# Layer 0's attention in a two-layer transformer trunk: fewer modulation blocks up to the latent heads, more beside the output product, and bias products and scores in another place of the order

## The chip, the cores and the metric

The kernel runs on one core of a Trainium2 chip. The metric is device time in microseconds of one launch; weights and activations come from the chip's memory in each launch. PE is the matrix engine (PEld its weight loads), DVE the vector engine, ACT the scalar engine, POOL the general one, SP the queue that issues the transfers.

## The reference

One sequence of 256 tokens of width 2048 goes through two layers, all in float32. A conditioning vector `c` gives each layer six vectors of 2048 (shift, scale and gate of the attention, shift, scale and gate of the MLP):

```python
cond = jax.nn.silu(c)
mod = cond @ w_ada[l] + b_ada[l]
sh_a, sc_a, g_a, sh_m, sc_m, g_m = split(mod, 6)
h = rmsnorm(x) * (1 + sc_a) + sh_a
proj = h @ w_in[l]          # dq, dk, dv (1024 each), cq 512, ckv 256, kr 64
out_a = diff_attention(dq, dk, dv, positions, bias_table, lam, ...)   # 4 heads, two softmaxes each, T5 bias
q  = rmsnorm(cq, gq) @ w_uq[l]      # 8 latent heads, 128 + 64 rotated
kv = rmsnorm(ckv, gkv) @ w_ukv[l]
out_b = mla_attention(q_nope, rope(q_rope), k_nope, rope(kr), v)
x = x + g_a * (concat(out_a, out_b) @ w_o[l])
h = rmsnorm(x) * (1 + sc_m) + sh_m
x = x + g_m * (square(relu(h @ w_mlp_in[l])) @ w_mlp_out[l])
```

A last norm ends it. `w_ada` is 2048 x 12288 per layer, 201 MB for both layers.

## The kernel before, in words

**Products.** Float32 weights are split on the way in: `weights()` loads one tile of 128 x 2048 (1 MB; a few are 128 x 1536) into one of five shared buffers `raw` (line 164), ACT copies it to `hi` in a reduced format (line 145) and DVE takes the rest, `lo` (line 146), half a tile at a time; `hi` and `lo` have four half-tiles each. A product is three passes, hi x hi, hi x lo, lo x hi (`mac`, lines 188 to 190; `tokens_by_k`, lines 259 to 261, with 512 columns a pass). Activations are split likewise. PSUM has eight banks, all from one pool.

**Modulation.** `w_ada` isn't multiplied on PE. It is cut into 192 blocks of 128 x 2048 (one block gives 128 outputs); a block is loaded into the same five `raw` buffers (`ada_load`, line 296), and one DVE pass multiplies it by the broadcast `cond` and sums the row (`ada_sums`, line 304). The blocks go in a fixed order `ada_todo`: layer 0's attention shift and scale (32), its gate (16), MLP shift and scale (32), MLP gate (16), then layer 1's in the same order. When they go is set by a *rate*: each call of `weights()` adds `self.rate` to a credit, and for each whole unit one block is loaded (`more`); its DVE pass is put behind the split of the next weight tile. In the softmax steps of layer 0's latent heads `tick` does the same with `RATE_S`. Where a value is needed and its blocks have not been loaded, `ada_need` loads and sums all up to it at that place.

**Layer 0.** `head` computes the norm and, in one loop over the 16 blocks of 128 features, the combined projection with `w_b` (latents, half of the queries and keys) into all eight PSUM banks; here the first 32 blocks of modulation are needed step by step (16 of them ahead of the loop). Products with the other queries, keys and the values were done for the first eight feature blocks before (`w_f1`, `w_v1`); `rest_feats` (`w_f2`) and `val(cg, 2)`, `val(cg, 3)` (`w_dv`) do the rest. Then, in `layer`: `latent` norms a latent; `bias_marks(a)` makes eight marks `oh` per query block a on ACT and DVE, and `bias_products(a, marks)` multiplies them by the bias table (lines 527, 528), for a = 2 and 3 here; `rope_setup` and `keys` make the rotated key; `probs(hd)` computes the two softmaxes of a differential head (scores at line 1041), `turn` transposes them; `up_k`, `up_q`, `up_r`, `up_v` are the products that go up from the latents. The list `mla` holds the three steps of each latent head (scores and softmax, transpose, values) in a staggered order, with a `tick` behind each of its ten groups. The output product follows: `w_oa` in four tiles, `w_ob` in twelve, then the norm and the product with `w_n0` (`norm_then_by_k`, 16 tiles in eight steps), then the MLP.

**What sets the order.** Each engine has one queue. Inside `manual_schedule(engines={PE})` PE's order is the written one: so in `head` and in the MLP. Elsewhere, so in all of layer 0's attention and its output product, a planner orders the instructions by simulated times, with the written order as its preference. Transfers are all issued from SP, in one order; a transfer into a `raw` buffer waits until the buffer's last reader on DVE is through.

Of the kernel before, what the change touches and what calls it, by code (L numbers as in the profile page):

```python
# [21 lines left out]
NK = D // P  # L22
# [71 lines left out]
NSPLIT = 8  # L94
# [3 lines left out]
NNORM = 12  # L98


RATE_H, RATE_A0, RATE_S, RATE_O, RATE_A1, RATE_A2, RATE_K, RATE_M = 1.25, 1.2, 1.3, 0.6, 0.5, 0.7, 0.6, 0.66


class Trunk:
# [261 lines left out]
    def head(self):  # L366
# [63 lines left out]
        self.part_v = [[flat(self.copy(ps, "pvp")) for ps in y] for y in vals]  # L430
        self.rate = RATE_H
        banks = self.open_banks(8)
        for k in range(NK):
            for i, w in enumerate(self.weights(io["w_b"][0, k])):
                for j in range(8):
                    b = 4 * i + j // 2
                    self.mac(banks[b][:, j % 2], w, j * P, P, h[k], k == 0 and j % 2 == 0, k == NK - 1 and j % 2 == 1, True)
            if k + 2 < NK:
                ready(k + 2)
        return h, banks  # L440

    def rest_feats(self, h, ps, banks):
# [262 lines left out]
    def layer(self, l, acc, st):  # L705
# [23 lines left out]
        def keys():  # L729
            ps = self.bank("pkr")  # L730
            self.tile_cols(ps[:, 0], io["w_kr"][l], h)
            self.kr = self.rope_k(ps[:, 0])

        def up_k():
            kn.extend(self.copy(ps, "kn") for ps in self.small(io["w_uk"][l], ckv, 8))

        def up_q(b):
            qn.extend(self.copy(ps, "qn", ms) for ps in self.small(io["w_uq"][l, b], cq, 4))
# [28 lines left out]
        def probs(hd):  # L767
            return lambda: a.append(self.diff_probs(l, hd, q[hd], kk[hd]))
# [15 lines left out]
        if l == 0:  # L784
            q += [self.copy(ps, "q", qs) for ps in banks[3:5]]
            kk += [self.copy(ps, "k", -1.0) for ps in banks[5:7]]
            q.append(self.copy(banks[7], "q", qs))
            ckv += self.latent([ckr], gkv)
            marks = self.bias_marks(2)
            banks = self.open_banks(3)  # L790
            self.rest_feats(h, (0, 1), banks)
            self.bias_products(2, marks)
            cq += self.latent(cqr, gq)
            marks = self.bias_marks(3)
            self.rope_setup()
            self.rest_feats(h, (2, 3), banks)
            k2, q3, k3 = self.rest_sums(banks)
            kk += [k2, k3]
            q.append(q3)
            self.bias_products(3, marks)  # L800
            self.lambdas()
            keys()
            probs(0)()
            up_k()
            probs(1)()
            for kq in (2, 3):
                val(0, kq)()
            probs(2)()
        else:
            def two(i, dst, scale):  # L810
                ps = self.wides([io["w_q"][0, i + j] for j in range(2)], h)
                dst.append(self.joined(ps, self.u("qk"), scale))

            two(0, q, qs)
            two(8, kk, -1.0)
            ckv += self.latent([ckr], gkv)
            for hd in range(1, HD):
                two(2 * hd, q, qs)
                probs(hd - 1)()
                two(8 + 2 * hd, kk, -1.0)  # L820
                if hd == 1:
                    cq += self.latent(cqr, gq)
            keys()
            self.rate = RATE_A2
            up_k()
        probs(3)()
        up_q(0)
        turn(0)()
        up_r()
        turn(1)()  # L830
# [6 lines left out]
        turn(3)()  # L837
        for f in mla[3:6]:
            f()
        self.interleave(  # L840
            [val(cg, kq) for cg in range(2) for kq in range(4)] if l else [val(1, kq) for kq in (2, 3)],
            mla[6:] + [av[0][0], av[1][0]],
        )
        acc = None
        g = self.mod[l, 2]
        self.ada_need(l, 2, NK - 1)
# [391 lines left out]
```

## Time and profile before

| what | value |
|---|---|
| median of 3 runs | 2251.49 us (2248.39 to 2251.86) |
| the profiled execution | 2249.45 us, its span 2247.6 us |
| PE busy | 2167.3 us, 96% of the span |
| DVE busy | 1627.8 us, 72% |
| ACT busy | 1153.5 us, 51% |
| `raw<-in_w_ada` blocks | 192 transfers of 1024 KB |
| one DVE pass over a block (line 304) | 2.28 us |
| all line 304 passes | 437.7 us of DVE |

A page of the profile shows one execution: busy times per engine, the span in forty slices, the chain of work that ended last, and groups of instructions by source line, written as output<-inputs. A wait is put down to the instruction whose semaphore came last. PE's busy time is modelled from pipelined instructions, so a full PE says that it never stood still, not that it ran at its peak.

### The profile page before, as it was taken

What the parts mean: (1) busy time and instruction counts of PE and PEld (TensorE: products, weight loads), DVE (VectorE), ACT (ScalarE), POOL (GpSimd) and SP (SyncE); (2) the same over time, 40 slices, a digit from 0 to 9 for tenths busy, and PEclk for the clock granted to TensorE, in tenths of its full rate; (3) what the DMA queues carried; (4) which work ended last, traced back from release to release, by engine and by line L of the source; (5) the groups of instructions that cost most, each with busy time, mean ns of one, the idle gap of its engine ahead of it and who ended that gap; (6) DMA issues with size and microseconds to landing.
All of it is one profiled execution on the core that took longest, in us unless ns stands there. A gap on an engine that the chain in (4) does not pass through costs nothing.

```text
span 2247.6 us, 31016 instructions
## 1 busy us (share of the span) xinstructions
PE 2167.3 (96%) x12318; PEld 1899.0 (84%) x12318; DVE 1627.8 (72%) x2168; ACT 1153.5 (51%) x1704; POOL 20.4 (1%) x43
## 2 busy tenths in 40 slices
PE   6996989999999999999999999999999999999997
PEld 4896768999888888888888888999888888888886
DVE  7898996798778777778799886678544545555555
ACT  3435546446455445445446655647545534544643
POOL 0000000000000000000001000000000000000000
PEclk9998889999999999999999999999999999999999
DMA  9897686778888888987877675675555554555551
GB/s 388 334 377 278 251 342 226 286 262 330 328 312 319 331 305 307 335 319 308 323 292 267 255 270 217 226 264 192 199 195 187 189 195 179 190 203 191 194 193 60
DMA packets 83811, 585.39 MB, mean 260 GB/s; under 512 B 9297, under 2 KB 9681, under 8 KB 17361
## 3 DMA queue, kind: packets, MB, share of 16 engines
q1 hardware_dynamic: 83666, 583.42, 69.7%
q8 instruction: 96, 1.57, 0.3%
q14 instruction: 49, 0.40, 0.0%
HBM read 581.28 MB, written 2.10 MB: 260 GB/s over the span
## 4 chain that ended last, share of the span: by engine, by line
PE 89%; DVE 7%; ACT 1%; DMA 1%; issue 1%; DVEq 0%; ACTq 0%; SPq 0%
PE ps L209 20%; PE ps L212 11%; PE py L941 10%; PE py L943 10%; PE py L939 10%; PE pk L190 2%; DVE ada L304 2%; PE pk L188 2%; PE pk L189 2%; PE ps L189 2%; PE ps L188 2%; PE ps L190 2%; DVE lo L146 1%; PE pv L259 1%; PE pv L260 1%; PE pv L261 1%
## 5 line engine op out<-in xcount | busy, mean ns | idle before, releaser
L146 DVE TENSOR_TENSOR lo<-raw,hi 128x1024 fp32r<-128x1024 f32 (+1 forms) x724 | 855.5, 1194 | 498.4 <-ACT hi L145 335.9
L145 ACT ACTIVATE hi<-raw 128x1024 fp32r<-128x1024 f32 (+1 forms) x724 | 745.4, 1036 | 708.9 <-PE py L943 373.1
L209 PE MATMUL ps<-h,hi 128*128 128x512 f32 x2016 | 472.8, 391 | 0.0
L209 PEld LDWEIGHTS ps<-h,hi 128*128 128x128 f32 x2016 | 375.1, 188 | 75.7
L304 DVE SCALAR_TENSOR_TENSOR ada<-ada,cond 128x2048 f32<-128x2048 f32 x192 | 437.7, 2282 | 0.0
L939 PE MATMUL py<-hi,hid 128*128 128x512 f32 x1024 | 326.0, 389 | 0.0
L941 PE MATMUL py<-lo,hid 128*128 128x512 f32 x1024 | 325.8, 389 | 0.0
L943 PE MATMUL py<-hi,hid 128*128 128x512 f32 x1024 | 325.7, 389 | 0.0
L212 PEld LDWEIGHTS ps<-h,lo 128*128 128x128 f32 x2016 | 250.5, 192 | 5.0
L212 PE MATMUL ps<-h,lo 128*128 128x256 f32 x2016 | 252.0, 283 | 0.0
L941 PEld LDWEIGHTS py<-lo,hid 128*128 128x128 f32 x1024 | 192.3, 188 | 40.1 <-DVE lo L146 0.4
L943 PEld LDWEIGHTS py<-hi,hid 128*128 128x128 f32 x1024 | 192.3, 188 | 39.9
L939 PEld LDWEIGHTS py<-hi,hid 128*128 128x128 f32 x1024 | 191.8, 188 | 39.2
L190 PE MATMUL pk<-h,lo 128*128 128x256 f32 x496 | 142.1, 288 | 6.9 <-DVE lo L146 6.7
L188 PE MATMUL pk<-h,hi 128*128 128x256 f32 x496 | 140.9, 286 | 3.4 <-ACT h L660 3.4
L189 PE MATMUL pk<-h,hi 128*128 128x256 f32 x496 | 141.6, 286 | 0.0
L190 PEld LDWEIGHTS pk<-h,lo 128*128 128x128 f32 x496 | 96.8, 196 | 7.9 <-DVE lo L146 7.7
L977 ACT ACTIVATE sum<-ps 128x256 f32<-128x256 f32 x110 | 42.1, 383 | 114.2 <-PE ps L212 113.6
L188 PEld LDWEIGHTS pk<-h,hi 128*128 128x128 f32 x496 | 96.2, 195 | 4.1 <-ACT h L660 3.8
L189 PEld LDWEIGHTS pk<-h,hi 128*128 128x128 f32 x496 | 96.7, 195 | 0.2
L182 DVE TENSOR_TENSOR hid<-relu,hid 128x256 fp32r<-128x256 f32 x128 | 48.3, 419 | 48.4 <-ACT hid L181 48.4
L190 PE MATMUL pa<-ah,lo 128*128 128x258 f32 x192 | 55.3, 288 | 4.6 <-DVE lo L146 4.6
(236 smaller groups left out, 2582.2 us busy)
## 6 DMA issues: line engine op xcount, KB each, us to landing
raw<-in_w_m SPq DMA_DIRECT2D x238, 1024.0 KB, 4.8
ada<-in_w_ada SPq DMA_DIRECT2D x192, 1024.0 KB, 5.0
raw<-in_w_ob SPq DMA_DIRECT2D x24, 1024.0 KB, 4.8
raw<-in_w_b SPq DMA_DIRECT2D x16, 1024.0 KB, 6.6
raw<-in_w_q SPq DMA_DIRECT2D x16, 1024.0 KB, 4.8
raw<-in_w_dv SPq DMA_DIRECT2D x12, 1024.0 KB, 4.8
raw<-in_w_n SPq DMA_DIRECT2D x16, 768.0 KB, 5.5
raw<-in_w_oa SPq DMA_DIRECT2D x8, 1024.0 KB, 5.4
```

The costliest lines, as they stand in the source:

```text
L145: nc.scalar.activation(hi, v, AF.Copy)
L146: ins = nc.vector.tensor_tensor(lo, v, hi.bitcast(F32), ALU.subtract)
L182: self.nc.vector.tensor_tensor(lo, val[:, i], hi.bitcast(F32), ALU.subtract)
L188: mm(ps, hi, x[0], start=first, stop=False, skip_group_check=shared)
L189: mm(ps, hi, x[1], start=False, stop=False, skip_group_check=shared)
L190: mm(ps, lo, x[0], start=False, stop=last, skip_group_check=shared)
L209: mm(ps.rearrange("p a b -> p (a b)"), part(w, 0, k), both, start=k == 0, stop=False)
L212: mm(ps[:, 0], part(w, 1, k), x, start=False, stop=k == nk - 1)
L304: ins = nc.vector.scalar_tensor_tensor(w, w, 1.0, self.cond, ALU.mult, ALU.mult, accum_out=acc[:, i : i + 1])
L939: mm(o, xh[:, tok], hi[:, part[j]], start=start, stop=False)
L941: mm(o, xh[:, tok], lo[:, part[j]], start=False, stop=False)
L943: mm(o, xl[:, tok], hi[:, part[j]], start=False, stop=stop)
```

## The change

It does five things.

- Rates: `RATE_A0` (layer 0's attention) from 1.2 to 0.35, `RATE_S` (ticks) from 1.3 to 0.75, `RATE_O` (its output product) from 0.6 to 1.1.
- In the head's loop the rate is set to zero once the first 32 blocks have been loaded.
- The first products after the head: `rest_feats` for the first two pairs goes ahead of the key latent's norm and the marks of query block 2; the bias product of block 2 goes behind the sums of `rest_feats`, and the query latent's norm and the marks of block 3 behind it.
- `val(0, 2)` and `val(0, 3)` go ahead of the marks' product of block 3, and `val(1, 2)`, `val(1, 3)` between the scores of the differential heads; `up_q(0)` goes between scores, too. So the last steps of the latent heads no longer have the two value products among them.
- For layer 1 nothing changes (the two lines for `probs(3)` and `up_q(0)` moved into its branch).

```diff
-RATE_H, RATE_A0, RATE_S, RATE_O, RATE_A1, RATE_A2, RATE_K, RATE_M = 1.25, 1.2, 1.3, 0.6, 0.5, 0.7, 0.6, 0.66
+RATE_H, RATE_A0, RATE_S, RATE_O, RATE_A1, RATE_A2, RATE_K, RATE_M = 1.25, 0.35, 0.75, 1.1, 0.5, 0.7, 0.6, 0.66
...
         banks = self.open_banks(8)
+        rest = len(self.ada_todo) - 2 * (NK - NSPLIT)
         for k in range(NK):
...
                 ready(k + 2)
+            if len(self.ada_todo) <= rest:
+                self.rate = 0.0
         return h, banks
...
             q.append(self.copy(banks[7], "q", qs))
+            banks = self.open_banks(3)
+            self.rest_feats(h, (0, 1), banks)
             ckv += self.latent([ckr], gkv)
             marks = self.bias_marks(2)
-            banks = self.open_banks(3)
-            self.rest_feats(h, (0, 1), banks)
-            self.bias_products(2, marks)
-            cq += self.latent(cqr, gq)
-            marks = self.bias_marks(3)
-            self.rope_setup()
             self.rest_feats(h, (2, 3), banks)
             k2, q3, k3 = self.rest_sums(banks)
             kk += [k2, k3]
             q.append(q3)
+            self.rope_setup()
+            self.bias_products(2, marks)
+            cq += self.latent(cqr, gq)
+            val(0, 2)()
+            marks = self.bias_marks(3)
+            val(0, 3)()
+            keys()
+            self.lambdas()
             self.bias_products(3, marks)
-            self.lambdas()
-            keys()
+            up_k()
             probs(0)()
-            up_k()
+            val(1, 2)()
             probs(1)()
-            for kq in (2, 3):
-                val(0, kq)()
+            up_q(0)
             probs(2)()
+            val(1, 3)()
+            probs(3)()
         else:
...
             up_k()
-        probs(3)()
-        up_q(0)
+            probs(3)()
+            up_q(0)
         turn(0)()
...
-        self.interleave(
-            [val(cg, kq) for cg in range(2) for kq in range(4)] if l else [val(1, kq) for kq in (2, 3)],
-            mla[6:] + [av[0][0], av[1][0]],
-        )
+        light = mla[6:] + [av[0][0], av[1][0]]
+        if l:
+            self.interleave([val(cg, kq) for cg in range(2) for kq in range(4)], light)
+        else:
+            for f in light:
+                f()
```

## The prediction

> **What bounds the kernel now.** I read the page's engine shares and its forty slices first, to see where the matrix engine is not full.
>
> ```profile
> span 2247.6 us, 31016 instructions
> PE 2167.3 (96%) x12318; PEld 1899.0 (84%) x12318; DVE 1627.8 (72%) x2168; ACT 1153.5 (51%) x1704; POOL 20.4 (1%) x43
> ...
> PE   6996989999999999999999999999999999999997
> DVE  7898996798778777778799886678544545555555
> PEclk9998889999999999999999999999999999999999
> ```
>
> PE works nearly everywhere but in slices 4 to 6 (some 170 to 340 us), where it falls to 6 tenths and its granted clock falls too, while DVE stands at 9. This is layer 0's attention. So I cut the time from 87 to 531 us at the stages' own borders (first to last product of each, from the order of time): the combined input projection to 182, attention to 355.4, output product to 457, the product with `w_n0` to 531. Columns: length, busy time (count) of PE, PEld, DVE, ACT, POOL, granted clock, DMA share, GB/s. The rows with one engine are those of line 304 alone, the pass that makes modulation from one block of `w_ada`; its count holds each pass and its read-out, so x64 is 32 blocks.
>
> ```profile
> 87.00:182.00 95.00, 92.90 (x768) 92.09 (x767) 83.21 (x99) 40.35 (x51) 0.00 (x0) 1.00 0.93 362
> 182.00:214.00 32.00, 25.29 (x168) 23.94 (x168) 30.58 (x42) 19.24 (x28) 0.00 (x0) 0.89 0.79 285
> 214.00:224.00 10.00, 0.00 (x0) 0.00 (x0) 10.00 (x19) 3.49 (x6) 0.00 (x0) 0.60 0.33 118
> 224.00:293.00 69.00, 57.47 (x308) 48.34 (x308) 64.24 (x133) 37.48 (x71) 0.81 (x1) 0.84 0.72 268
> 293.00:355.40 62.40, 52.53 (x262) 44.40 (x262) 57.71 (x100) 34.87 (x80) 0.00 (x0) 0.95 0.84 322
> 386.00:457.00 71.00, 70.66 (x581) 69.75 (x579) 54.31 (x64) 29.90 (x35) 0.00 (x0) 1.00 0.78 282
> 457.00:531.00 74.00, 70.67 (x576) 70.67 (x577) 63.88 (x89) 37.20 (x56) 0.00 (x0) 0.98 0.80 291
> 182.00:355.40 173.40, 135.30 (x737) 116.68 (x738) 162.53 (x291) 95.08 (x183) 0.81 (x1) 0.87 0.75 282
> ...
> 182.00:355.40 173.40, 73.02 (x64) 0.87 0.75 282
> 386.00:457.00 71.00, 16.05 (x14) 1.00 0.78 282
> 457.00:531.00 74.00, 20.63 (x18) 0.98 0.80 291
> ```
>
> Attention takes 173.4 us, in which DVE works 162.5 (94%) and PE 135.3. Of DVE's time 73.0 us are the 32 blocks, which this stage does not need: 2.28 us each. In the output product PE is full and DVE has 17 us to spare; in the product with `w_n0` it has 10. The list of waits between 181 and 355.4 us says what PE stood for (us, times, longest):
>
> ```profile
> PE pb L527 <- DVE oh L516: 11.2, 1, 11.2
> PE pk L190 <- DVE lo L146: 6.0, 1, 6.0
> PE psm L1108 <- DVE qr L1019: 4.9, 1, 4.9
> PE psc L1041 <- DVE mx L1042: 4.7, 3, 3.6
> PE pqr L1014 <- ACT qr L278: 4.0, 1, 4.0
> PE pt L1059 <- ACT sm L1112: 3.3, 2, 3.0
> ```
>
> Nearly all end in DVE. The longest is the bias product of query block 3: its marks (`oh`) come after the latent's norm on DVE, and no other product is at hand. The clock costs as well: busy time by granted clock over the four parts is 25.3 x 0.89 + 57.5 x 0.84 + 52.5 x 0.95 = 121 us at full clock, against 135.3.
>
> **The change, part by part.** *How many blocks move.* The rates add up call by call in the code. Before, the head's 16 weight tiles at 1.25 issue 20 blocks; the attention's 14 tiles at 1.2 and ten ticks at 1.3 issue 29 (three of the head's are summed here, which makes the 32 seen). After, the head stops at 16; 14 x 0.35 + 10 x 0.75 with a credit of 0.25 issue 12, and `ada_need(0, 2, 15)` ahead of the output product forces the four still missing of its gate: 16. Output product: 16 tiles at 0.6 give 10, at 1.1 they give 18. The `w_n0` stage: 9 by rate in both, but only 18 of the 32 blocks of shift and scale are there when it starts, so the last two of its eight steps force three each: 15.
>
> *Attention, DVE.* 162.5 - 73.0 + 16 x 2.29 = 126 us. *PE* at full clock is 121. So the bound is no longer one engine, and what counts is how the two overlap. The end of the stage I take by itself, because `val(1, 2)` and `val(1, 3)` no longer run between its heads. The stretch before the output product where that is already so:
>
> ```profile
> 331.00:350.00 19.00, 14.38 (x72) 11.61 (x71) 16.84 (x38) 14.71 (x36) 0.00 (x0) 0.98 0.77 297
> ...
> 331.00:350.00 19.00, 7.73 (x8) 0.98 0.77 297
> ...
> 332.71 0.59 PE L1107 MATMUL psm<-kn,qn 128*128 128x256 f32 x2
> ...
> 344.81 0.59 PE L1107 MATMUL psm<-kn,qn 128*128 128x256 f32 x2
> ```
>
> From the first to the seventh of these half-head scores are 12.1 us, so 4.0 us a head, with 7.7 us of blocks (3.4 passes) in 19 us: about what the new rate issues. Five heads have their scores in the new tail: 20 us, and from the last score (344.8) to 355.4 another 10. Tail: 30 us, with PE busy 23 of them and DVE 27, by this row's shares. The four forced blocks come in the tail too, 9.2 us of DVE ahead of the first `w_oa` split: nothing if they fit the drain, 9.2 if they all delay it; I take 5, the middle, since DVE has only 11% free in that row. What is left for the stage ahead of the tail is PE 121 - 23 = 98, DVE 126 - 27 - 9 = 90. With 10% for waits (before, DVE, the bound then, lost 7%, and now both are close) 108. Sum 108 + 35 = 143, against 173.4: **-30 us**. Ends: perfect overlap, 98 + 30 = 128, gives -45; if only the first two waits of the list go, -17.
>
> *The moved order.* Marks, bias products, norm of the query latent and scores each get a product behind which they can wait: the 11.2 us of `pb` is covered by `val(0, 2)` and the rest products. Cover gone, that wait comes back. Only in the head does PE follow the written order; in this section a planner lays out the instructions by simulated times, so the written order is no more than a preference. It is priced inside the 10%. `probs(3)` and `up_q(0)` in the other branch stay where they were: nothing for layer 1.
>
> *Head.* Four blocks fewer at its end. PE is idle 2.1 of 95 us there; the wait of 6.0 right after it, for a weight tile that was late, is inside the attention's sum. -1 us (0 to -2).
>
> *Output product.* From 386 to 457 are 12 tiles: 13 blocks instead of 7 make DVE 54.3 + 6 x 2.29 = 68 of 71 us. Its transfers grow to 25 of 1024 KB in 71 us, some 370 GB/s. The nearest rows for such density are the head's own 87 to 182 (20 blocks beside 16 tiles) and its middle:
>
> ```profile
> 60.00:80.00 20.00, 20.00 (x73) 13.64 (x72) 14.55 (x23) 6.03 (x12) 0.00 (x0) 1.00 1.00 419
> 120.00:155.00 35.00, 35.00 (x294) 35.00 (x294) 30.64 (x39) 12.24 (x14) 0.00 (x0) 1.00 0.97 387
> ...
> raw<-in_w_n SPq DMA_DIRECT2D x16, 768.0 KB, 5.5
> ...
> ada<-in_w_ada SPq DMA_DIRECT2D x192, 1024.0 KB, 5.0
> ```
>
> PE was full over 35 us at 387 GB/s, and 419 was reached. The head's idle 2.1 and the late tile's 6.0 make 8 the upper end; 0 is the lower, and I take **+3**, nearer the full row because this density is a little lower. The five shared buffers of tiles and blocks are the link: a later block waits on SP for DVE to free one, and the next tile is queued behind it.
>
> *`w_n0` stage.* 63.9 + 6 x 2.29 = 77.6 us of DVE in 74: 3.6 over. And they are not spread: without blocks a step costs DVE (63.9 - 20.6) / 8 = 5.4, with 4.2 blocks 15.0, against 70.67 / 8 = 8.8 of PE, so 6.2 over in each of the last two, 12 together, less what DVE is ahead (two tiles' worth, at most 8.8). Between +3 and +12, I take **+6**, nearer the plain excess of 3.6. In bytes: 12.6 MB of `w_n` and 15 blocks, 28.3 MB in 74 us, 382 GB/s, under both rows above.
>
> The Trainium skill says otherwise: in "DMA: Bandwidth & Descriptors", section "Where 436 GB/s comes from", transfers from HBM are held to about 358 GB/s per core. By that figure the two stages' 64 MB would need 179 us instead of 175.6, so 3 us more, and the sum would be -19 and the time 2232 us. The two rows above, 387 and 419, do not agree with it, and I leave it out of the sum.
>
> *Later stages.* Three blocks fewer are done when the MLP starts; its rate of 0.66 is the same, no need is missed, and the three are made up in layer 1's output product, where blocks now run on at the same rate for some tiles longer than before. A row of that place:
>
> ```profile
> 1470.00:1500.00 30.00, 30.00 (x253) 30.00 (x252) 25.35 (x29) 13.01 (x14) 0.00 (x0) 1.00 0.82 297
> ```
>
> PE is full there with blocks running, so 0; without that cover 3 x 2.29 = 7 us.
>
> **Sum.** -30 - 1 + 3 + 6 = -22 us. Span 2247.6 to 2225.6. The profiled execution took 2249.45, so 2227; the runs' median, 2251.49, lies 2.0 above that, and less 22 it gives **2229 us**.
>
> **Rivals.**
> (1) *More is won*: the two engines overlap nearly fully, -40 to -45, and the later stages give back only 5. For it: layer 1's attention, at a rate of 0.5, with its four value products between the heads:
>
> ```profile
> 1306.00:1420.00 114.00, 113.21 (x649) 98.47 (x648) 82.50 (x137) 65.55 (x122) 0.00 (x0) 1.00 0.64 239
> ```
>
> PE idles 0.8 of 114 us. Against: DVE is at 72% there, here it would be near 90%. Time 2212.
> (2) *Waits take the place of waits*: the bias marks or the rotated queries stay late, the bare tail goes chain-bound with the clock dropping (0.60 where PE stood still). The stage gains the lower end's 17, the later stages cost 9: 2243. For it: 16.9 us of the waits listed are on scores, rotation and softmax, and a block still stands ahead of them on DVE now and then.
> (3) *Slower: the blocks cost more where they go than they did here.* In the output product and `w_n0` stage a block stands between two weight splits on DVE, the tile behind it waits for a buffer, PE waits for the tile. It decides from a loss of 31 us over 32 tiles, 1.0 us a tile; at 1.3 a tile the time is 2262. For it: DVE at 96% and more in both. Against: the head, as dense, lost 8.1 over 16 tiles, half a microsecond a tile.
> (4) *It does not do what it says*: the planner puts products and marks back as they were. Then the order is worth nothing, but 16 blocks fewer still shorten DVE's queue; it ends in (2), or, with more given back, within 4.5 us of before.
>
> **How the numbers follow.** Likeliest case (2215 to 2237) 0.55; rival 1 0.13; rival 2 with 4's first half 0.17; no change, within 0.2% (4.5 us, about what a measurement of this kernel tells from no change) 0.05; slower 0.10. Hence faster 0.85. The range from 2211 to 2247 holds the likeliest case, rival 2 and about half of rival 1.
>
> **What would show it.** Right: attention about 143 us with 16 blocks of line 304 in it, the `pb` wait gone, granted clock above 0.95; PE idle a few us in the output product; an idle stretch of PE in the last two steps of `w_n0`, waiting for `lo` or `h`. Wrong: attention still above 155 us with PE waiting on softmax or rotation; PE idle over 15 us between the output product's first tile and the MLP; or a DMA share of 1.0 with PE waiting there.

## The result, and the profile after

The changed kernel takes 2253.68 us (median; 2252.25 to 2257.56) against 2250.93 for the kernel before on the same chip: ratio 1.0014, 95% interval 1.0008 to 1.0021. That is inside the 0.2% which the prediction called no change. It forecast 2229 with a range of 2211 to 2247, so the measured time lies outside. The profiled execution took 2253.18 us.

The page of the kernel after, the lines that answer to those shown of before (TensorE is PE in the rows, VectorE DVE, ScalarE ACT):

```profile
span 2251.4 us, 31003 instructions
PE 2173.8 (97%) x12318; PEld 1899.5 (84%) x12318; DVE 1628.3 (72%) x2168; ACT 1152.5 (51%) x1704; POOL 17.8 (1%) x43
...
PE   6998989898999999999999999999999999999997
DVE  7886987898777877777899886688544545555555
PEclk9998999999999999999999999999999999999999
```

Slice 4 has risen from 6 to 8 tenths of PE, but slices 8 and 10 (394 to 450 and 507 to 563 us), which stood at 9, are at 8. Busy time by stage (columns as in the prediction; first all engines, then line 304 alone, whose count is twice the blocks):

```profile
182.00:340.20 158.20, 134.20 (x733) 111.69 (x731) 127.91 (x250) 92.81 (x179) 0.81 (x1) 0.91 0.58 213
340.20:451.00 110.80, 102.87 (x814) 100.52 (x812) 91.44 (x113) 49.13 (x79) 0.00 (x0) 0.97 0.81 295
451.00:532.40 81.40, 74.05 (x577) 73.15 (x578) 73.30 (x97) 35.15 (x54) 0.00 (x0) 0.94 0.89 341
505.00:532.40 27.40, 20.37 (x145) 19.67 (x146) 24.14 (x33) 12.75 (x22) 0.00 (x0) 0.88 1.00 401
...
182.00:340.20 158.20, 38.86 (x34) 0.91 0.58 213
340.20:451.00 110.80, 38.85 (x34) 0.97 0.81 295
451.00:532.40 81.40, 34.15 (x30) 0.94 0.89 341
```

The later two stages before, cut at the same events (first `w_oa` product, first `w_n0` product, first wide product of the MLP):

```profile
355.40:460.30 104.90, 101.25 (x814) 99.12 (x812) 74.46 (x94) 50.05 (x78) 0.00 (x0) 1.00 0.69 251
460.30:531.00 70.70, 70.67 (x576) 70.67 (x577) 61.08 (x86) 36.24 (x54) 0.00 (x0) 0.98 0.81 293
```

The attention (182 us to the first `w_oa` product) is 15.2 us shorter. The output product with its norm gives back 5.9, the `w_n0` stage 10.7, and what follows is 2.4 longer (1719.0 against 1716.6): -15.2 + 5.9 + 10.7 + 2.4 = +3.8, the difference of the spans. What TensorE waited for in the kernel after, first between 181 and 340 us, then between 340 and 533:

```profile
PE pn L588 <- DVE acc L579: 5.8, 1, 5.8
PE psm L1117 <- DVE qr L1028: 4.8, 1, 4.8
PE psm L1116 <- DVE sm L1118: 4.5, 5, 1.6
PE pb L530 <- DVE oh L519: 4.2, 4, 2.6
...
PE pk L188 <- ACT h L663: 10.1, 3, 5.0
PE ps L188 <- ACT hi L145: 2.6, 1, 2.6
```

(`pn` is the product that sums a norm's squares, `pb` the bias product, `psc` the scores of the differential heads, `psm` those of the latent heads, `pk` in the second list the product with `w_n0`.) The 11.2 us wait for marks is down to 4.2. A new one stands at the top: the query latent's norm (`pn`). In the later stages TensorE waits for `h`, the modulated activations: 3.4 of the 10.1 us stand at the norm ahead of `w_n0`, as before the change, and 6.7 in the last two steps.

### The profile page after: what moved, and what is told of

Same layout as the page of the kernel before. It is cut to its first block, busy times and chain, and to the rows that moved or that the text cites. A ratio compares the mean times of both kernels' runs of the same rounds, so it can differ in the third digit from the quotient of the medians.

```text
span 2251.4 us, 31003 instructions
## 1 busy us (share of the span) xinstructions
PE 2173.8 (97%) x12318; PEld 1899.5 (84%) x12318; DVE 1628.3 (72%) x2168; ACT 1152.5 (51%) x1704; POOL 17.8 (1%) x43
## 4 chain that ended last, share of the span: by engine, by line
PE 86%; DVE 9%; ACT 2%; DMA 1%; issue 1%; DVEq 0%; ACTq 0%
PE ps L209 20%; PE ps L212 11%; PE py L950 10%; PE py L948 10%; PE py L952 10%; DVE ada L304 4%; PE ps L188 2%; PE ps L189 2%; PE ps L190 2%; DVE lo L146 2%; PE pk L189 2%; PE pk L190 2%; PE pk L188 2%; PE pv L259 1%; PE pv L261 1%
## 5 line engine op out<-in xcount | busy, mean ns | idle before, releaser
L188 PE MATMUL pk<-h,hi 128*128 128x256 f32 x496 | 141.5, 288 | 10.1 <-ACT h L663 10.1
```

The costliest lines, as they stand in the source:

```text
L188: mm(ps, hi, x[0], start=first, stop=False, skip_group_check=shared)
```

## The experiments

The stages of each run in us, cut as above, with the blocks summed in each; ratios are to the kernel before on the same chip. A star marks kernels that cut blocks short, so that parts of their sums are left out. The stages come from the one profiled execution of each kernel, the times are medians; the two can differ by some us (the profiled execution of e1 took 2253.0, of e18 2250.2, of e5 2258.2).

| run | attention (blocks) | output + norm (blocks) | `w_n0` (blocks) | sum | time | ratio, 95% |
|---|---|---|---|---|---|---|
| before | 173.4 (32) | 104.9 (9) | 70.7 (9) | 349.0 | 2250.9 | 1 |
| after | 158.2 (17) | 110.8 (17) | 81.4 (15) | 350.4 | 2253.7 | 1.0014 (1.0008-1.0021) |
| e1 | 176.9 (32) | 104.7 (9) | 70.8 (9) | 352.4 | 2256.8 | 1.0025 (1.0016-1.0034) |
| e2 | 154.0 (17) | 111.7 (17) | 82.2 (15) | 347.9 | 2248.5 | 0.9992 (0.9983-1.0001) |
| e3 | 161.3 (17) | 110.8 (17) | 81.6 (15) | 353.7 | 2256.2 | 1.0026 (1.0017-1.0035) |
| e8 | 155.9 (17) | 111.7 (17) | 82.4 (15) | 350.0 | 2253.2 | 1.0016 (1.0007-1.0025) |
| e14 | 164.8 (17) | 110.9 (17) | 82.3 (15) | 358.0 | 2260.9 | 1.0050 (1.0036-1.0064) |
| e22 | 152.5 (17) | 111.8 (17) | 82.1 (15) | 346.4 | 2250.2 | 1.0005 (0.9996-1.0014) |
| e16* | 148.8 (5, 12*) | 110.8 (17) | 82.5 (15) | 342.1 | 2245.1 | 0.9975 (0.9966-0.9984) |
| e23* | 143.3 (5, 12*) | 111.8 (17) | 82.3 (15) | 337.4 | 2240.5 | 0.9963 (0.9949-0.9976) |
| e4* | 158.1 (17) | 110.2 (17*) | 79.6 (15*) | 347.9 | 2250.6 | 1.0003 (0.9994-1.0012) |
| e17* | 155.6 (17) | 105.3 (17*) | 79.2 (15*) | 340.1 | 2246.7 | 0.9979 (0.9970-0.9988) |
| e10* | 158.8 (17) | 104.8 (17*) | 71.9 (15*) | 335.5 | 2236.3 | 0.9942 (0.9930-0.9955) |
| e5 | 160.5 (17) | 114.0 (18) | 80.7 (14) | 355.2 | 2255.3 | 1.0027 (1.0017-1.0037) |
| e18 | 168.2 (22) | 105.9 (15) | 73.6 (10) | 347.7 | 2246.6 | 0.9981 (0.9972-0.9990) |
| e19 | 174.4 (22) | 105.8 (15) | 71.2 (10) | 351.4 | 2252.2 | 1.0006 (0.9997-1.0015) |
| e20 | 161.7 (15) | 118.1 (21) | 81.6 (13) | 361.4 | 2266.1 | 1.0077 (1.0065-1.0090) |
| e21 | 166.2 (19) | 110.9 (17) | 70.6 (10) | 347.7 | 2251.5 | 1.0009 (1.0000-1.0018) |
| e24 | 164.7 (23) | 104.7 (15) | 76.3 (11) | 345.7 | 2248.3 | 0.9993 (0.9984-1.0002) |
| e25 | 172.1 (23) | 104.7 (15) | 74.4 (11) | 351.2 | 2254.0 | 1.0021 (1.0011-1.0031) |

**The two halves of the change.** e1 has the new order with the rates of before and no stop in the head's loop; e2 has the order of before with the new rates and the stop.

```diff
 # e1, on the kernel after
-RATE_H, RATE_A0, RATE_S, RATE_O, ... = 1.25, 0.35, 0.75, 1.1, ...
+RATE_H, RATE_A0, RATE_S, RATE_O, ... = 1.25, 1.2, 1.3, 0.6, ...
-        rest = len(self.ada_todo) - 2 * (NK - NSPLIT)
...
-            if len(self.ada_todo) <= rest:
-                self.rate = 0.0
 # e2, on the kernel before: the same lines the other way round
```

> The written order of the changed kernel with the rates of before (32 blocks in the attention again, head not stopped). Theory A (the order as such costs or wins little, the blocks were what filled DVE): DVE has its 162 us of work in the attention again, the stage takes 170 to 176 us, the time is within 5 us of before. Theory B (the new order by itself removes late waits): the 11 us wait of the bias product goes although DVE is full, the stage takes about 162, the time is about 2240. Theory C (the new order makes a stall of its own where the bias product of block 2 and the query latent's norm stand ahead of the values on PE): the stage takes 178 or more, the time 2255 or more.

> The old written order with the new rates and the head's stop (16 blocks in the attention, 33 in the two stages behind it). Theory C (the new order stalls at 199 to 220 us, some 15 us of loss): without it the attention takes 145 to 150 us instead of 158, the stages behind lose their 16 as in the changed kernel, time 2241 to 2247. Theory A: attention 156 to 160, time 2251 to 2256 as in the changed kernel. Theory B: the bias product's wait of 11 us is back, attention 165 or more, time 2260.

Measured: the order alone costs 3.5 us in the attention, and the rates with the stop alone gain 19.4, so the order takes 4.2 us back from the rates. e1's attention lies between its theories A and C, with the time of C; e2 lies between C and A. By the times e1 is 0.25% slower than before, and e2 cannot be told from before. In e1 the wait that tops the list between 181 and 358 us is the one that is new in the kernel after, and the wait for marks is down from 11.2:

```profile
PE pn L585 <- DVE acc L576: 12.3, 1, 12.3
...
PE pb L527 <- DVE oh L516: 3.3, 4, 1.0
```

e2 has no wait of `pn` for `acc`, but keeps most of the wait for marks. Its attention, and the first line of its list:

```profile
182.00:336.00 154.00, 132.81 (x742) 113.83 (x741) 127.34 (x250) 93.01 (x181) 0.67 (x1) 0.92 0.60 220
...
PE pb L530 <- DVE oh L519: 8.2, 1, 8.2
```

So the order covers the marks and opens a wait of its own. The later stages pay nearly the same with either order: 111.7 and 82.2 in e2, where the order is that of before.

**Why the new order waits.** ScalarE's order of time in the kernel after shows the place:

```profile
210.87 0.63 ACT L575 ACTIVATE acc<-cqr 128x512 f32<-128x512 f32 x1 [5.63 <-PE pb L531]
211.82 2.39 ACT L533 ACTIVATE bias<-pb 32x512 f32<-32x512 f32 x4 [0.31 <-PE pb L531]
214.22 1.28 ACT L559 ACT_TABLE_LOAD   x1
215.52 0.42 ACT L559 ACTIVATE sin<-rr 128x256 f32<-128x256 f32 x1
215.84 0.40 ACT L560 ACTIVATE cos<-cc 128x256 f32<-128x256 f32 x1
216.15 0.62 ACT L578 ACTIVATE sqx<-cqr 128x512 f32<-128x512 f32 x1
216.78 1.28 ACT L590 ACT_TABLE_LOAD   x1
```

The norm's first square waits 5.6 us for the bias product, which gives back a buffer; its second square stands behind the copy of the bias, a table load and the angles' sine and cosine. e3 puts `val(0, 2)` first, e8 the angles behind the marks of block 3, e14 the angles and the rotary keys ahead of the query latent's norm:

```diff
 # e3: val(0, 2) first, val(0, 3) behind the bias product of block 2
+            val(0, 2)()
             self.rope_setup()
             self.bias_products(2, marks)
+            val(0, 3)()
             cq += self.latent(cqr, gq)
-            val(0, 2)()
             marks = self.bias_marks(3)
-            val(0, 3)()
 # e8: the angles later
-            self.rope_setup()
             self.bias_products(2, marks)
...
             marks = self.bias_marks(3)
+            self.rope_setup()
 # e14: rope_setup behind the key latent's norm, and after rest_sums:
+            keys()
             cq += self.latent(cqr, gq)
+            marks = self.bias_marks(2)
             val(0, 2)()
+            self.bias_products(2, marks)
             marks = self.bias_marks(3)
```

> The changed kernel with val(0, 2) ahead of the bias product of block 2 and val(0, 3) ahead of the query latent's norm. Theory C (PE stands at 199 to 220 because the products that could run are queued behind those two): 11 us of products fill the stall, the clock isn't dropped there, attention 144 to 148, time 2240 to 2245. Rival: DVE's chain of marks, angles and norm is what takes that long, and PE will wait for its end wherever the values stand: attention 156 to 160, time within 3 us of the changed kernel.

> The changed kernel with one line moved: rope_setup (the angles, their sine and cosine) stands behind the marks of head 3 instead of ahead of the query latent's norm. Theory A (the angles' chain on VectorE and the sine, cosine and table loads on ScalarE stand ahead of the norm's second square, and TensorE's queue waits at the norm's pn product): the 5.8 us wait of pn for acc goes, the half-clock stretch at 199 to 220 us shrinks, the attention ends 6 to 10 us earlier and the kernel takes 2243 to 2248. Rival B (the first square and the marks wait for a buffer that the bias product gives back, wherever the angles stand): the wait for pb or pn stays at 5 us or more in another place, the angles are then late for the rotary query product, and the time stays within 3 us of the changed kernel, 2251 to 2256.

> The changed kernel with the angles and the rotary keys (a product over eight tiles of h, which frees h's buffers) ahead of the query latent's norm, then norm, marks of head 2, values 2, bias products 2, marks 3, values 3. Theory B (u buffers hold the marks and the first square back): with h given back early the marks and the squares run ahead of TensorE, waits for pb, acc and oh at 195 to 225 us sum to under 4 us instead of 11, and the attention ends 8 to 12 us earlier: 2241 to 2247. Theory A alone (ScalarE's queue order): the norm now stands behind the sine and cosine as before, and the wait at pn stays at 5 us or more: 2250 to 2256. A third outcome, a wait moved to the keys product for the angles (8 us of chain on VectorE): a wait at krt or pk of 5 us, 2250 to 2255.

In e3 and e14 the repair failed: attention 161.3 and 164.8, with `pn` waiting 9.7 and 11.2 us. That is near e3's rival; in e14 the wait at `pn` stayed, as "A alone" says, but the time is above its range. e8 removed the wait as its theory A says, and yet gained only 2.3 us, with the time of rival B. Its list for the attention:

```profile
PE psm L1116 <- DVE sm L1118: 5.6, 4, 2.6
PE psc L1050 <- DVE mx L1051: 4.9, 3, 2.5
PE psm L1117 <- DVE qr L1028: 4.4, 1, 4.4
PE pb L530 <- DVE oh L519: 4.2, 4, 2.6
...
PE pn L588 <- DVE acc L579: 0.5, 1, 0.5
```

The 5.3 us gone from `pn` are back as 4.5 more at `psc` (0.4 in the kernel after) and 1.1 more at `psm`. TensorE stands as long as before the repair (24.6 us of the attention against 24.0); the 2.3 us come out of its busy time, 131.3 us at a clock of 0.93 against 134.2 at 0.91. The later stages are 1.9 us longer besides, so the kernel's time is that of the kernel after. e22 adds to e8 the other suspect, the buffers:

```diff
-            oh = half("oh", F32R)
+            oh = self.ap.tile([P, 2 * TX], F32R, tag="a", name=self.name("oh"))[:, : 2 * T] if a >= 2 else half("oh", F32R)
```

> The run with the angles later, with the marks of heads 2 and 3 in a pool of six tiles that is idle there, instead of among the 40 u tiles. Theory buffers (marks and first square wait for tiles that the bias product gives back): the 4.2 us wait of pb for oh and part of the later ones go, attention 150 to 153 us instead of 155.9, kernel 2245 to 2249. Rival VectorE (the marks wait for their turn on VectorE and ScalarE, not for a tile): attention within 2 us of 155.9, kernel 2250 to 2255.

The attention went from 155.9 to 152.5, the length that "buffers" gives, so marks did wait for tiles, in part. But `pb` still waits 3.4 us for marks, and the time, 2250.2, lies in the rival's range. With both repairs the new order is 1.5 us better there than the old one (e2), which was not run with marks in that pool; the sum of stages is 4.0 below the kernel after, and the time cannot be told from before.

**What the blocks still cost in the attention.** e16 (on the kernel after) and e23 (on e8) cut the transfer and pass of blocks in the attention from 2048 to 256 columns. As run, that was 12 of the 17; the five at its end stayed whole, so VectorE had 22 us less to do and not the 32 that the expectation counts.

```diff
+        n = 256 if self.short else D
-        self.nc.sync.dma_start(w, self.io["w_ada"][l, NK * g + i])
+        self.nc.sync.dma_start(w[:, :n], self.io["w_ada"][l, NK * g + i][:, :n])
...
-                w, w, 1.0, self.cond, ALU.mult, ALU.mult, accum_out=acc[:, i : i + 1]
+                w[:, :n], w[:, :n], 1.0, self.cond[:, :n], ALU.mult, ALU.mult, accum_out=acc[:, i : i + 1]
```

> The changed kernel with the 17 modulation blocks that the attention of layer 0 loads cut to 256 of 2048 columns, transfer and pass (their sums are left out to 7/8). VectorE has 17 x 1.87 = 32 us less to do between 182 us and the end of the attention. Theory load (the waits of TensorE that are left stand behind blocks on VectorE, so moving still more of them out would go on paying 1.2 us a block): the attention goes from 158.2 us to 138 to 143, kernel 2233 to 2238. Rival latency (what is left are chains of short steps on VectorE and ScalarE, marks, angles, norm, rotary query, softmax, which wait for one another with or without blocks): the attention stays at 151 to 158, the waits at pn and psm are as before, kernel 2246 to 2253.

> The run with the angles later, with the attention's 17 blocks cut to 256 columns as in the run that had the angles early (there 148.8 us with 6.0 us of wait at pn and 8.4 at the latent heads' scores; the sums of these blocks are left out to 7/8). Theory place (with VectorE light, the wait at pn is the angles' alone): pn's wait under 1.5 us and the attention 141 to 145, kernel 2236 to 2241. Rival latency (the wait goes to the next short chain, as it did with whole blocks, where 5.3 us of wait gone bought 2.3): attention 146 to 149, kernel 2241 to 2246.

```profile
182.00:330.80 148.80, 128.00 (x729) 109.19 (x728) 105.89 (x250) 92.42 (x179) 0.69 (x1) 0.94 0.43 158
```

The row is e16's. It lies between the two forecasts: 9.4 us less than in the kernel after, with VectorE busy for 105.9 of 148.8 us, 71%. The waits at `pn` and `psm` are still there (6.0 and 8.4 us). e23 met "place": with VectorE light, moving the angles is worth 5.5 us (148.8 to 143.3) instead of 2.3. So in the kernel after the chains of short steps and the blocks hide one another in part: 2.3 and 9.4 us one by one, 14.9 together.

**What the later stages pay for.** On the kernel after, in the output-product and `w_n0` stages only: e4 cuts the passes (edit as above, without the transfer), e10 passes and transfers, e17 the transfers, with VectorE kept busy:

```diff
 # e17: transfers as in e10, and
+            for _ in range(5 if self.short else 1):
+                ins = nc.vector.scalar_tensor_tensor(w[:, :n], w[:, :n], ...)
```

> The changed kernel, but in the output product and the w_n0 stage each DVE pass over a modulation block takes 256 of its 2048 columns (so shift, scale and gate of the MLP lack the rest of their sums); all transfers stay. If DVE's time is what these stages lose: w_n0 goes from 81 to 71-73 us, output product with its norm from 111 to 105, time 2237 to 2241. If it is the transfers (DMA share 1.00 in the last two steps): w_n0 stays at 78 or more, time 2249 or more.

> The changed kernel with the transfers of the modulation blocks and their passes on VectorE cut to 256 of 2048 columns in the output-product and w_n0 stages (it leaves out 7/8 of the sums of those blocks, so the time tells only what the rest takes). Theory: the blocks' transfers and passes together are the whole loss of the two stages: output product and norm back to 104 to 106 us, w_n0 to 70 to 72 us, kernel 2251 less 14 to 18: 2234 to 2239. Rival (part of the loss is the clock or the order of TensorE's products, not the blocks): the stages stay at 108 or more and 76 or more, kernel 2243 to 2250.

> The changed kernel with the blocks' transfers in the output-product and w_n0 stages cut to 256 of 2048 columns, and VectorE kept as busy as before with five passes of 256 columns (2.5 us a block against 2.37; the sums of those blocks are left out to 7/8). With short passes alone the two stages fell by 2.4 us, with both short by 15.3 us. Theory transfers (the loss of both stages is the queue's time for 32 blocks of 1 MB): output product and norm 104 to 107 us, w_n0 71 to 75 us, kernel 2236 to 2242. Rival either (transfers and VectorE each hold the stage at the same length, so that only both together give it back): 109 and 79 us or more, kernel 2248 to 2253.

Output product and `w_n0`, e4:

```profile
340.10:450.30 110.20, 102.95 (x814) 100.69 (x812) 61.30 (x113) 49.24 (x79) 0.00 (x0) 0.97 0.77 295
450.30:529.90 79.60, 74.03 (x576) 73.36 (x577) 47.18 (x99) 34.02 (x52) 0.00 (x0) 0.93 0.85 338
```

e10:

```profile
340.80:445.90 105.10, 101.43 (x815) 99.42 (x814) 62.72 (x114) 50.68 (x80) 0.00 (x0) 1.00 0.53 178
445.90:517.50 71.60, 71.60 (x577) 71.60 (x577) 47.55 (x98) 34.72 (x52) 0.00 (x0) 0.96 0.60 208
```

e17:

```profile
337.60:442.90 105.30, 101.12 (x814) 99.06 (x812) 85.44 (x241) 50.62 (x79) 0.00 (x0) 0.99 0.52 178
442.90:522.10 79.20, 74.02 (x577) 73.61 (x578) 65.31 (x203) 35.57 (x54) 0.00 (x0) 0.93 0.58 199
```

(e10's first border between the two stages is 0.3 us late; at the first `w_n0` product they are 104.8 and 71.9.) With both short the stages are back at the lengths of before within 1.2 us, so the blocks are nearly the whole loss. In the output product it is the transfers: passes alone give back 0.6 us, transfers alone 5.5, with VectorE busy for 85.4 us (91.4 in the kernel after). In the `w_n0` stage either alone holds it near 79 us; only both together give it back, so there e17's rival was right. With short passes the wait in its last steps is 5.5 us for `hi`, the split of a weight tile (e4); with short transfers it is 5.1 us for `h` (e17, where VectorE has 65.3 us of work and not 73.3).

e5 asks whether spreading helps there (on the kernel after):

```diff
-            self.rate = RATE_K
+            self.rate = RATE_K if l else 1.0
```

> The changed kernel with one number changed: in the w_n0 stage of layer 0 the blocks go at 1.0 for each product instead of 0.6, which spreads the blocks that the changed kernel forces in the last two of its eight steps evenly over all eight. Theory lump (the loss of 10.7 us in this stage is that six blocks fall on two steps): the stage goes from 81.4 to 72 to 75 us, the 6.7 us of waits for h by the modulation vanish, kernel 2245 to 2249. Rival total (the stage has 30 blocks' transfers and passes whatever their place, 341 GB/s on the mean and 0.89 of the transfer engines' time): waits spread over the eight steps, stage 78 us or more, kernel 2251 to 2255.

The lump theory fell: 80.7 us with 14 blocks spread, and in the last quarter of the stage TensorE still waits 4.2 us for `h`. From 483 us on, that is for two thirds of the stage, its transfers stand at 0.96 to 0.98.

**Rates between.** e18 (order of before) and e19 (order of e8) leave the head unstopped and lie between the two sets of rates; e20 and e21 vary e18; e24 is e18 with the stop, e25 is e22 with the rates of e24.

```diff
 # RATE_A0, RATE_S, RATE_O, then the rate in layer 0's w_n0 stage
 # e18, e19:  0.65, 1.05, 0.95   0.65   no stop
 # e20:       0.35, 0.75, 1.35   0.9    no stop
 # e21:       0.65, 0.75, 1.1    0.65   no stop
 # e24, e25:  0.8,  1.15, 0.95   0.65   stop
```

> The kernel before with rates between: RATE_H not stopped (four blocks more beside w_b, as before), RATE_A0 0.65, RATE_S 1.05, RATE_O 0.95, and 0.65 in the w_n0 stage of layer 0, for about 20 blocks in the attention, 15 at the output product and 11 at w_n0 instead of 32, 9, 9 and 17, 17, 15. Theory convex (a stage takes some blocks free, up to what its transfers and VectorE have spare, and only the blocks past that cost: w_n0 took 9 for nothing and the next 6 cost 10.7 us): attention 154 to 158, output product 106 to 109, w_n0 71 to 74, kernel 2236 to 2243, faster than both. Rival linear (a block costs about the same wherever it goes, 0.6 to 1.8 us): the sum stays at 2247 to 2252.

> The changed order with the angles behind the marks of head 3, and the same rates between as in the run with the old order. Theory convex: attention 156 to 160 us, output product 106 to 109, w_n0 71 to 74, kernel 2238 to 2246; the old order is equal or 2 us better, since the new one pays 2 to 4 us at marks and norm. Rival linear: 2249 to 2254.

> The order of before, RATE_H not stopped, the low rates of the change in the attention (0.35 and 0.75), 1.35 at the output product and 0.9 in w_n0: about 15 blocks in the attention, 20 at the output product, 14 to 15 in w_n0, with 69 to 71 of the 80 in by the start of w_n0, where the changed kernel had 66 and the run with the rates between 71. Theory due (h of step 7 needs the last block at about step 5, so what counts is how many are missing at the start): w_n0 73 to 76 us, output product 110 to 114, attention 152 to 156, kernel 2242 to 2246. Rival count (w_n0 pays for each block that falls in it): 79 to 82, kernel 2248 to 2252.

> The order of before with RATE_A0 0.65 as in the run with the rates between (attention 168.2 us with 22 blocks), but RATE_S 0.75 as in the changed kernel, RATE_O 1.1 and 0.65 in w_n0: about 20 blocks in the attention, three fewer of them beside the latent heads. Theory start (the step between 17 blocks and 22 lies beside the products up to the bias, where TensorE waited 8.8 us for marks and 6.0 for a lo half): attention 164 to 168, the waits for oh and lo stand, kernel 2246 to 2250. Rival end (it lies beside the heads, where RATE_S counts): attention 155 to 159, kernel 2238 to 2243.

> The order of before with RATE_H stopped as in the change, RATE_A0 0.8, RATE_S 1.15, RATE_O 0.95 and 0.65 in w_n0: about 22 blocks in the attention, 15 at the output product, 11 in w_n0. Theory stop (the blocks beside the last products of w_b delay the first lo half and the marks; a block later in the attention costs 0.5 to 0.9 us): the 6.0 us wait of pk for lo is gone, attention 157 to 161 us, output product 105 to 107, w_n0 71 to 74, kernel 2235 to 2241, the fastest so far that computes everything. Rival number (the step lies between 17 and 22 blocks whatever the stop): attention 165 to 170, kernel 2244 to 2250.

> The changed order with the angles later and the marks of heads 2 and 3 in the idle pool (152.5 us of attention with 17 blocks), RATE_H stopped, and the rates of the other run of this pair. Theory stop: attention 156 to 160 us, output product 105 to 107, w_n0 71 to 74, kernel 2234 to 2241. Rival number: the attention is at 165 us or more, as with the rates between in this order (174.4 without the stop), kernel 2244 to 2252.

e18 is faster than both kernels, by 0.19% (0.10 to 0.28) of the kernel before, but its attention missed by 10 us, e19's by 14, and neither time is in the range of "convex". The two later stages behaved nearly as "convex" says (105.9 and 73.6, 105.8 and 71.2), and e20 and e21 sharpen it. Output product and `w_n0`, e20:

```profile
343.70:461.80 118.10, 105.12 (x815) 102.24 (x813) 95.86 (x118) 49.12 (x79) 0.00 (x0) 0.96 0.80 297
461.80:543.40 81.60, 75.29 (x577) 72.96 (x577) 72.25 (x102) 36.13 (x60) 0.00 (x0) 0.95 0.91 331
```

e21:

```profile
348.20:459.10 110.90, 103.00 (x814) 100.56 (x812) 91.36 (x113) 49.10 (x79) 0.00 (x0) 0.97 0.79 296
459.10:529.70 70.60, 70.57 (x577) 70.58 (x578) 62.17 (x87) 35.45 (x54) 0.00 (x0) 0.98 0.86 321
```

Over all runs with whole blocks the output stage takes 104.7 to 105.9 us with 9 to 15 blocks, 110.8 to 111.8 with 17, 114.0 with 18, 118.1 with 21; `w_n0` takes 70.6 to 76.3 with 9 to 11 and 80.7 to 82.4 with 13 to 15. One by one, `w_n0` has 70.6 to 73.6 with 9 or 10 blocks, 74.4 and 76.3 with 11, and about 81 to 82 from 13 on. The "due" theory of e20 fell: e20 and e21 start `w_n0` with equally many blocks in (70 of 80) and differ by 11 us there; what differs in the stage is its rate, with 13 against 10 blocks. e20's rival "count" has the stage right, but not the time, since the output product took 118.1 us.

In the attention no price per block holds. e21's "start" was right for the attention (166.2), though the time is 1.5 us above its range: the waits for a `lo` half and for marks stand, as in e18, whose first rows are these:

```profile
PE pb L527 <- DVE oh L516: 8.8, 1, 8.8
PE pk L190 <- DVE lo L146: 6.0, 1, 6.0
PE psm L1108 <- DVE qr L1019: 5.4, 1, 5.4
```

Every run without the stop in the order of before has the 6.0; e2 and e24, with it, do not. e20 takes 161.7 us with 15 blocks unstopped, e2 154.0 with 17 stopped, so the stop is worth some 8 us there. But e24, stopped, with 23 blocks, is at 164.7 instead of the 157 to 161 expected, 3.5 better than e18: six blocks more than in e2 cost 10.7 us (1.8 each), where from 15 to 22 without the stop they cost 6.5 (0.9 each), and from 22 to 32 (e18 to before) 5.2 (0.5 each). e24 and e25 thus missed (their `w_n0` too, 76.3 and 74.4), and the rival "number" is nearer. With as many blocks the new order, with the angles later, is 6 to 7 us longer than the old one (e19 against e18, e25 against e24): there `psc` waits 9.9 and 14.6 us for the maximum of a softmax on VectorE (`mx`), against 4.9 in e8. Why a block costs 0.5 us at one count and 1.8 at another stays open.

## Why the prediction was wrong, point by point

**Its own signs of being wrong came.** The attention is above 155 us, with waits at the rotated queries and softmax (4.8 and 4.5 us); TensorE stands 7.9 + 7.4 = 15.3 us between the output product's first tile and the MLP; and the transfer share is 1.00 in the last two steps of `w_n0`, with TensorE waiting there.

**Block counts and loads were right.** 17, 17 and 15 blocks against 16, 18 and 15 worked out (one falls past a border); VectorE 127.9 us in the attention against 126; TensorE 134.2 x 0.91 = 122 at full clock against 121.

**The attention term failed: -15.2 instead of -30, 14.8 of the 25.8 us by which the span differs.** The step is "with 10% for waits ... 108". Cut at the last product up from the latents, the kernel after has:

```profile
182.00:310.50 128.50, 109.10 (x607) 91.80 (x606) 110.50 (x207) 71.34 (x126) 0.81 (x1) 0.89 0.59 215
310.50:340.20 29.70, 25.10 (x128) 19.88 (x126) 17.41 (x46) 21.47 (x54) 0.00 (x0) 1.00 0.53 204
```

The tail came out near its 30 us (29.7, and the 5 for forced blocks did not come), in part by luck: it holds the scores of six heads and not of five, and VectorE works 17.4 us in it, where the sum has 27 + 9 = 36. The blocks ran earlier than the sum has them: 15 of the 17 stand ahead of the tail, 34.2 us of line 304, where the sum leaves 36.6 - 12.2 - 9.2 = 15 (its row's 7.7 us in 19 give 12.2 for 30). So "DVE 126 - 27 - 9 = 90" failed as well: it is 110.5, more than the 108 us that the sum gives to all of that part. TensorE has 109.1 x 0.89 = 97 us of work at full clock there, as predicted (98), but the part takes 128.5: 19.4 us idle and 12 lost to the clock, 32% over TensorE's work and 16% over VectorE's, and not 10%. The 10% was taken from a stage in which one engine was the bound. Here no engine is full and the queues wait for one another, and it does not hold: e16 stays at 148.8 us even with VectorE at 71%, and 143 us, the predicted length, was reached only by e23, with 12 blocks cut short and the angles moved.

**"Priced inside the 10%": the moved order.** It got no price of its own, and has one. The order costs 3.5 us at the old rates (e1) and 4.2 at the new (e2 against the kernel after). "The 11.2 us of `pb` is covered" was right in itself, 4.2 being left, where the rates alone leave 8.2 (e2). What is late next was not looked for: the query latent's norm, whose second square now stands on ScalarE behind the sine, the cosine and a table load, and whose first waits for a buffer. That the planner might put all back (rival 4) did not happen.

**Head, -1: not seen.** By the count of its products the head ends at 180.6 us before and about 181.0 after. But the stop has its effect just after that border, the 6.0 us wait that the prediction named and put "inside the attention's sum".

**Output product, +3: measured +5.9.** The range of 0 to 8 held it; the value was too near the full row. Fifteen blocks would have been nearly free (105.9 us in e18, 104.7 in e24), the next two cost 5 to 6 us, and it is the transfers (e4, e17).

**`w_n0` stage, +6: measured +10.7, within the 3 to 12.** The waits are where the prediction said, in the last two steps (TensorE 20.4 of 27.4 us), so 7.0 us idle, and the clock in that row, 0.88, takes 20.4 x 0.12 = 2.4 more. The reason was half of it. A lump on VectorE was forecast; with its passes cut the stage still takes 79.6 (e4), spread it takes 80.7 (e5), since the transfers are full at the same place (share 1.00, 401 GB/s); with the transfers cut and not the passes it takes 79.2 (e17). The term took the larger of two mean loads; both were near the limit, and the mean over the stage hid it.

The Trainium skill's figure, in "DMA: Bandwidth & Descriptors", section "Where 436 GB/s comes from", would by the prediction's estimate have added 3 us. That addition is wrong: the 179 us are a least length for both stages, and the sum already has 175.6 + 9 = 184.6 for them, so the figure would have added nothing. The two stages cost 7.6 us more than forecast. The 401 GB/s over 27.4 us are above its 358, so that ceiling was not the one met. The Trainium skill's "Perfetto Trace Analysis", section "Roofline", gives a core that is active alone about 435 instead, which the rows here don't exceed. That the transfers cost the output product its time was borne out (e4, e17).

**Later stages, 0: measured +2.4.** It goes with the rates and not with the order: that part takes 1716.6 us before, 1716.8 in e1 and 1719.1 in e2. Over all kernels here it spreads from 1716.6 to 1721.0; what in it takes the 2.4 us is left open.

**The rivals.** Rival 2 had the attention (17 gained, 15.2 measured) but 9 given back instead of 16.6. Rival 3 had the place of the loss; its price came to 16.6 / 32 = 0.5 us a tile, half of what it needed, and its mechanism, passes that keep a buffer from the next tile, is not what the runs show: in the output product the passes' share is 0.6 us (e4), and in `w_n0` TensorE waits for `h`.

**A reading.** Only slice 4 of the page falls to 6 tenths of TensorE; slices 5 and 6 are at 9 and 8. The slow clock, 8 tenths, is in all three.

**One account of it, not shown.** Cutting the blocks short in the attention gave 9.4 us (e16), in the later stages 110.8 + 81.4 - 104.8 - 71.9 = 15.5 us (e10): together 25. Before, the later stages took 9 + 9 blocks at the lengths that e10 shows almost without them (104.9 and 70.7 against 104.8 and 71.9), and the attention stood 173.4 - 148.8 = 24.6 us above e16, which has another order. By this account the change spread over three stages a cost of about 25 us that had stood in one. But e10 and e16 were not run as one kernel, and e16 shortens 12 blocks of 17. In 12 of the 15 kernels with whole blocks the sum of the three stages lies between 345.7 and 353.7 us.

## What to carry to other kernels

Here work that fills gaps was nearly free in a stage up to a count, and past it cost about its transfer or pass. The output product took 15 blocks so and then lost 2 to 3 us a block up to 21; `w_n0` took 9 or 10 and lost some 10 us from there to 13, and no more up to 15. A pass with its read-out takes 2.37 us, and 1 MB at the 401 GB/s of the full row 2.6. So before moving such work, find that count for the stage that receives it, from the busiest stretch of its transfers and VectorE and not from their means. And where a stage's bound is removed, do not size it by the next engine's load and a few per cent: list, for each in-order queue, what now stands ahead of each short step that the matrix engine needs.

## What the hardware showed that was not expected

The granted clock is lower where the gaps are. In the kernel after, the 21 us around the norm's wait have TensorE busy 11 us at 0.65, and with that wait gone (e8) 16 us at 0.76. What the clock takes is the same in both, 11.05 x 0.35 = 16.29 x 0.24 = 3.9 us, so in this stretch the wait cost its own length and no more. The kernel after, then e8:

```profile
199.00:220.00 21.00, 11.05 (x25) 6.10 (x24) 15.57 (x33) 13.11 (x20) 0.00 (x0) 0.65 0.30 110
```

```profile
199.00:220.00 21.00, 16.29 (x53) 10.62 (x52) 15.17 (x27) 13.02 (x20) 0.00 (x0) 0.76 0.31 115
```

The Trainium skill's "TensorE: Matmul & The Clock Gate", section "Part 1: The HAM clock gate", has the clock fall to half after an idle window of some 3.4 us; the two rows agree with it in direction, as mixtures of full and half, and no run here shows the window's length.

The two table loads on ScalarE, to the sine and back to the square root, take 1.28 us each, on a queue that the norm needs. "ScalarE activation tables: per-element evaluation and per-set limits" in the Trainium skill, section "What a function is on this engine", has the same 1283 ns; what was not expected is where they stood.
